# Two transformer blocks on one core: side work ordered by estimated readiness, and 64-row score products

## The chip, the cores and the metric

The kernel is one program on one NeuronCore of a Trainium2 chip. The metric is device time in microseconds (us) of one execution. The engines are called as in the profile: PE (TensorE, matrix products), PEld (its weight loads), DVE (VectorE), ACT (ScalarE), POOL (GpSimd), SP (SyncE, which only issues transfers here). A product has a stationary operand of up to 128 x 128 and a moving one of up to 512 columns; the result goes to a bank of PSUM.

## The reference, cut to what matters

Batch 1, 256 positions, width 2048, two different blocks, one after the other:

```
h = rms_norm(x)                       # block 1
aq, ak, av, hq, hf, hi, hg, gate_a, gate_b = split(h @ w_in)
y_attn = sliding_window_attention(rotary(aq), rotary(ak), av, sinks)  # 16 heads of 64, 4 kv heads, window 128
o = rms_norm(hgrn2_recurrence(silu(hq), hf, hi)) * silu(hg)           # 8 heads of 128
x = x + rms_norm((sigmoid(gate_a)*(y_attn@w_ab) + sigmoid(gate_b)*(o@w_hb)) @ w_out)
x = x + rms_norm((silu(gate) * up) @ w_down)                          # gate, up = rms_norm(x) @ w_gate_up
x = x + rms_norm((p @ w_ple_proj) * sigmoid(rms_norm(x) @ w_ple_gate))

proj = rms_norm(x) @ w_in_2           # block 2
score = sum over 16 index heads of w * relu(q_idx . k_idx / 8)        # heads of 64, top 64 keys of each row
a = softmax over the chosen keys, in a latent of 256                  # dsa, 8 heads of 128
b = causal softmax with a decay from cumulated log gates              # fox, 8 heads of 128
x = x + concat(a, b) @ w_o
x = rms_norm(x + conv_ffn(rms_norm(x)))
```

In the local attention a row of the first 128 positions sees 128 keys, a row of the second 128 sees 256, of which the window masks half. All inputs and results are fp32.

## The kernel before

**The main stream.** The large matrices are read in pieces of 512 KB (two times 128 rows by 512 columns) by transfers that SP issues. For each piece ACT rounds the numbers to the type fp32r (L283) and DVE forms what the rounding left off (L289); both go into a page called `ring`. A result tile (a bank named `mm`, 128 positions by 512 columns) is the sum of three products for each 128 rows of the matrix: rounded by rounded, rounded by rest, rest by rounded, all at L335 in `step`. `run` lays out in advance a list of steps of six such products each, gives each a planned time, and issues them one by one; the pieces of `ring` are made by a planned lead of about 12 us.

**The side work.** Everything between the large matrices (norms, rotary, local attention `swa`, the recurrence `hgrn`, gates, the indexer `head_iq`, `dsa`, `fox`) is written as Python generators. After each 1.4 us of planned time `run` calls `pump`, which advances every generator that is due by one piece. `yield 7` means "go on seven calls later". Nothing is reordered afterwards: the order in which the instructions are issued by this program is their order on each engine. So the yields decide where on PE a side product stands: an engine works its instructions in that order and waits where an operand is missing. Side products write to one of four banks named `sd`. They are plain fp32; transposes are done on PE too, against an identity matrix (`ident`).

**The waits.** All waits of the side work are fixed numbers of calls: `SWA_LEAD` 7, `Y_SOFT` 7 (between the softmax and the transposes of its result), `B_LEAD` 1, `FLIP_OUT` 5 and `FLIP_IN` 10 (around a turn of a tile through memory in the two feed-forward parts), and single numbers 2 to 7 elsewhere. Where the main stream itself needs a result of the side work that isn't yet written, `pump_until` calls `pump` until it is there.

**Local attention.** `swa` works one pair of heads after another, eight pairs. The keys are kept in `kz`, transposed, padded with zeros so that a product over all 128 rows gives one head of the pair in one half of its columns and the other in the other half: L626 gives the scores of the first 128 positions (256 columns for the pair), L627 of the second (512 columns). DVE scales and masks (L630, L632), takes maxima; ACT exponentiates; DVE divides by the sum (L653). After `Y_SOFT` calls six transposes (L660 to L662), two copies by ACT (L663, L664), and after three calls more the product with the values (L670 over 512 columns, L671 over 256), where each head uses one half of the result's rows.

**The indexer.** `head_iq` does the same for 16 index heads with one shared key: 16 blocks of one product each (256 or 512 columns), one bank and one ACT instruction for each, then DVE adds.

**Other lines.** L350 is a set of four transposes, L400 the evacuation that multiplies by a gain and rounds, L491 and L507 are small set-up products, L612 a copy of transposed queries. In `hgrn` L814 forms sums of logs on PE, L817 and L820 (POOL, 512 columns) and L821 (DVE) make its two operands, L827 uses them. L1349 gives the scores of `dsa` and `fox` in `softmax_pv`, L1352 their evacuation; L1244 is a set of transposes of block 2; L1428 cumulates the log gates from `nbf` (L1424). L963 and L997 lie at the end of the third large product of block 1, where the sum of squares of a whole row must be there before the next matrix can start.

## Time and profile before

| | us |
|---|---|
| median of 3 runs | 2660.38 |
| lowest and highest of them | 2657.01, 2662.94 |
| the profiled execution, its own time | 2657.43 |
| its span, first to last instruction | 2655.6 |
| PE busy in it | 2623.4 (99%) |
| DVE, ACT, POOL busy | 1613.8, 1339.5, 361.8 |

The granted clock of PE over the profiled execution was 0.998 of full speed. PE holds 11929 product records; one plain fp32 product is two records (it is done in two passes with two loads of weights), one fp32r product is one. A record's end is modelled and reaches past the start of the next; the time that a product takes is read from the start of one record to the start of a later one.

### The profile page before, as it was taken

The page shows a single profiled execution, that of the slowest core. Times are in us where ns is not written, and L with a number is a line of the kernel's source. Part 1 is how long each engine was busy: PE and PEld are TensorE (multiplying, and loading weights), DVE is VectorE, ACT ScalarE, POOL GpSimd, SP SyncE. Part 2 cuts the span into 40 slices and gives each one's busy share as a digit, 9 for nine tenths or more (in the row PEclk, how much of TensorE's full clock was granted, in tenths as well). Part 3 has the DMA queues.
Part 4 walks back from the last instruction along what each step waited for, and adds up shares of the span by engine and source line. Part 5 has one row for each costly group of instructions (what it writes and reads, how often), then busy time and mean ns, then how long its engine had stood idle before and what let it go on. Part 6 is the DMA issues. An engine that isn't in the chain of part 4 may idle for free.

```text
span 2655.6 us, 32471 instructions
## 1 busy us (share of the span) xinstructions
PE 2623.4 (99%) x11929; PEld 2168.9 (82%) x11929; DVE 1613.8 (61%) x2145; ACT 1339.5 (50%) x2004; POOL 361.8 (14%) x420
## 2 busy tenths in 40 slices
PE   8999999999999999999999999999999999999998
PEld 7887788888888888888887788788888888888887
DVE  6765676465555454545457564855557757575757
ACT  6545654454553443443435574554556636464644
POOL 1341031020100000000001110100013212121211
PEclk9999999999999999999999999999999999999999
DMA  7545445666676565656566666456556766575754
GB/s 256 165 129 171 161 147 185 221 230 243 219 243 219 212 210 206 217 201 223 209 209 220 235 213 184 137 175 214 191 198 235 250 221 237 209 242 207 246 202 146
DMA packets 154431, 547.02 MB, mean 206 GB/s; under 512 B 19512, under 2 KB 22096, under 8 KB 153248
## 3 DMA queue, kind: packets, MB, share of 16 engines
q1 hardware_dynamic: 133504, 476.83, 51.9%
q0 software_dynamic: 19472, 67.54, 7.8%
q8 instruction: 93, 1.52, 0.2%
q10 hardware_dynamic: 1296, 0.59, 0.1%
q14 instruction: 66, 0.54, 0.1%
HBM read 514.46 MB, written 30.43 MB: 205 GB/s over the span
## 4 chain that ended last, share of the span: by engine, by line
PE 95%; ACT 1%; DVE 1%; POOL 1%; issue 1%; DMA 0%; SPq 0%; ACTq 0%; POOLq 0%; DVEq 0%
PE mm L335 89%; PE sd L350 1%; PE sd L827 1%; DVE ring L289 1%; ACT ring L283 0%; PE sd L1272 0%; PE sd L1349 0%; POOL s L820 0%; ACT s L394 0%; PE sd L670 0%; PE sd L1381 0%; PE sd L627 0%; PE sd L1244 0%; DMA s<-in_x_dram 0%; PE sd L813 0%
## 5 line engine op out<-in xcount | busy, mean ns | idle before, releaser
L335 PE MATMUL mm<-ring,s 128*128 128x512 f32 (+1 forms) x10824 | 2508.7, 391 | 8.0 <-ACT ring L283 6.3
L335 PEld LDWEIGHTS mm<-ring,s 128*128 128x128 f32 x10824 | 2023.4, 188 | 430.8 <-ACT ring L283 7.6
L289 DVE TENSOR_TENSOR ring<-stg,ring 128x1024 fp32r<-128x1024 f32 (+1 forms) x904 | 1088.9, 1252 | 406.2 <-ACT ring L283 399.4
L283 ACT CAST ring<-stg 128x1024 fp32r<-128x1024 f32 (+1 forms) x904 | 904.5, 1049 | 159.3 <-PE mm L335 93.8
L370 POOL DMA_DIRECT2D flip<-s x66 | 37.0, 562 | 973.0 <-DVE s L366 967.4
L1231 ACT ACTIVATE s<-mm,ss 128x512 f32<-128x512 f32 x60 | 41.5, 691 | 237.6 <-PE mm L335 224.9
L1068 DVE TENSOR_TENSOR s<-mm,s 128x512 f32<-128x512 f32 x72 | 48.7, 687 | 86.5 <-PE mm L335 86.3
L1020 ACT ACTIVATE s<-mm,ss 128x512 f32<-128x512 f32 x22 | 15.2, 690 | 139.1 <-PE mm L335 139.1
L1033 DVE SCALAR_TENSOR_TENSOR s<-mm,ss,s 128x512 f32<-128x512 f32 x22 | 16.1, 730 | 108.3 <-PE mm L335 108.3
L345 POOL TENSOR_TENSOR small<-small,mhalf 128x1 f32<-128x1 f32 (+1 forms) x27 | 17.5, 649 | 361.3 <-DVE small L344 328.7
L820 POOL TENSOR_TENSOR s<-s,s 128x512 f32<-128x512 f32 x32 | 53.3, 1672 | 93.8 <-ACT s L817 89.1
L356 ACT CAST s<-sd 64x256 fp32r<-64x256 f32 (+2 forms) x34 | 16.0, 470 | 88.6 <-PE sd L350 49.7
L376 POOL DMA_DIRECT2D s<-flip x66 | 50.5, 767 | 67.8 <-DMA flip<-s 39.8
L394 ACT ACTIVATE s<-sd,cols 128x128 fp32r<-128x128 f32 x160 | 45.8, 388 | 22.0 <-PE sd L350 19.1
L357 DVE TENSOR_TENSOR s<-s,s 128x512 fp32r<-128x512 f32 x22 | 15.2, 690 | 65.3 <-ACT s L356 65.3
L1584 POOL TENSOR_TENSOR s<-s,s 128x512 f32<-128x512 f32 x22 | 41.2, 1874 | 82.9 <-DVE s L1567 82.8
L350 PE MATMUL sd<-ident,s 128*128 128x128 f32 x252 | 40.8, 285 | 9.9 <-DMA ident<-in_c_ident_dram 4.0
L350 PEld LDWEIGHTS sd<-ident,s 128*128 128x128 f32 x252 | 32.4, 147 | 20.7 <-DMA ident<-in_c_ident_dram 4.0
L1565 ACT ACTIVATE s<-s,cols 128x256 f32<-128x256 f32 x88 | 48.2, 594 | 1.5
L357 DVE TENSOR_TENSOR s<-sd,s 64x256 fp32r<-64x256 f32 (+2 forms) x34 | 18.7, 549 | 47.4 <-ACT s L356 47.3
L1587 ACT CAST s<-s 128x512 fp32r<-128x512 f32 x22 | 13.6, 620 | 66.7 <-POOL s L1584 66.7
L366 DVE STREAM_TRANSPOSE s<-s 128x512 f32<-128x512 f32 x66 | 46.2, 706 | 1.6
(293 smaller groups left out, 1247.4 us busy)
## 6 DMA issues: line engine op xcount, KB each, us to landing
stg<-in_w_in_dram SPq DMA_DIRECT2D x232, 512.0 KB, 4.4
stg<-in_w_gu_dram SPq DMA_DIRECT2D x176, 512.0 KB, 5.5
stg<-in_w_dn_dram SPq DMA_DIRECT2D x176, 512.0 KB, 5.4
stg<-in_w_up_dram SPq DMA_DIRECT2D x176, 512.0 KB, 5.3
flip<-s POOLq DMA_DIRECT2D x66, 256.0 KB, 2.6
s<-flip POOLq DMA_DIRECT2D x66, 256.0 KB, 5.7
stg<-in_w_out_dram SPq DMA_DIRECT2D x32, 512.0 KB, 5.7
stg<-in_w_pg_dram SPq DMA_DIRECT2D x32, 512.0 KB, 5.5
```

What stands on the lines that cost most here:

```text
L283: nc.scalar.copy(w[:, 0, :, 0 : cc.n], stg[n_hi][0][:, :, 0 : cc.n])
L289: nc.vector.tensor_tensor(wl[:, :, 0 : cc.n], unstage(n_lo)[:, :, 0 : cc.n], wh[:, :, 0 : cc.n].bitcast(F32), op=ALU.subtract)
L335: nc.tensor.matmul(c.ps[t][:, 0 : c.n], xl if p == "C" else xh, wl if p == "B" else wh, start=n == 0, stop=n == 6 * c.nhp - 1)
L350: self.nc.tensor.transpose(bank[:, a * P : (a + 1) * P], s, self.ident)
L366: nc.vector.transpose(ts, src)
L376: self.mq.dma_start(tr.rearrange("p (i x) -> p i x", i=4), d.rearrange("(i r) (j x) -> (r j) i x", i=4, j=4))
L394: nc.scalar.activation(hi[:, a], b3[:, a], AF.Copy, scale=g[a])
L820: nc.gpsimd.tensor_tensor(k3, d3, kt[:, None, :].to_broadcast([P, 4, P]), op=ALU.mult)
L1068: nc.vector.tensor_tensor(y, ps[t], y, op=ALU.add)
L1231: nc.scalar.activation(r, ps[t], AF.Copy, scale=self.rs[t])
L1565: nc.scalar.activation(v, u, AF.Identity, scale=w[2], bias=self.cols[:, C_CB + k : C_CB + k + 1])
L1584: nc.gpsimd.tensor_tensor(o, o, g, op=ALU.mult)
```

## The change

1. **Order by estimate.** Three new classes wrap the engines. While the program is issued they add up a cost for each instruction and keep, for each piece of a tile, an estimated time when it is written and read. A generator that used to yield a fixed number now yields 1 and then stays in `ripe(operands)` until the estimate for its operands is at most 0.3 us (`RIPE`) past the estimated time of PE (or of the engine named). `get("sd")` likewise waits until a bank is estimated free. Two ways around it: before the end of the set-up (`early`), and when the main stream has asked for a result for more than two calls (`rush`).
2. **Local attention in rounds of two pairs.** `kz` has no padding. A head's scores are a product over its own 64 rows; each pair has four products (128, 128, 256, 256 columns) into two banks. Two pairs follow each other, then all their 12 transposes into three banks, three ACT copies, and the product with the values as four products, each into 64 rows of the result, then one evacuation for both pairs.
3. **The indexer.** The same over 64 rows: one block of eight products of 128 columns and two of four products of 256 columns, for each half of the heads; six blocks instead of 16.
4. **Smaller.** No zeros are written and six transposes of padded keys are gone; two small transfers of `hgrn` are issued earlier; `softmax_pv` takes its two banks for transposes at once.

```
+RIPE = 0.3
+PATIENCE = 2
+class Watched:
...
+    def cost(self, op, out, ins, kw):
+        n = max(a.size() // max(1, a.shape[0]) for a in [out, *ins])
+        if op == "dma_start":
+            return (0.5, 1.9, out.size() * 4 / 340e3) if self.name == "SP" else (0.5, 4.3)
+        if self.name == "PE":
...
+                return n / 2400 + 0.0134 + back, 0.25
...
+            return (0.109 if op == "transpose" else 2 * max(0.109, r.size() // r.shape[0] / 1200)), 0.25
+        if self.name == "ACT":
+            return 0.15 + n / 1280 + (0.19 if "accum_out" in kw else 0.0), 0.15
+        if self.name == "DVE":
+            return 0.13 + n / 960, 0.15
+        return 0.3 + n / 450, 0.2
...
     def get(self, cls, n=1, dt=F32):
-        while not self.can(cls, n):
+        while not self.can(cls, n) or (cls == "sd" and not (self.rush or self.early) and not self.clk.free(cls, n)):
             yield 1
...
+    def ripe(self, *aps, eng="PE"):
+        while not (self.rush or self.early) and max(self.clk.there(a) for a in aps) > self.clk.now(eng) + RIPE:
+            yield 1
...
-            nc.tensor.matmul(p0, qt[:, 0:P], kz[:, q, :, 0:P], start=True, stop=True)
-            nc.tensor.matmul(p1, qt[:, P:256], kz[:, q, :, :], start=True, stop=True)
...
+                for t in range(2):
+                    for a, rows in enumerate(halves):
+                        nc.tensor.matmul(banks[a][:, P * t : P + 256 * t], qt[rows, P * t : P * t + P],
+                                         kz[rows, q, 0 : P + P * t], start=True, stop=True)
...
-            yield Y_SOFT
...
+            yield from self.ripe(l0, *l1)
...
-            nc.tensor.matmul(bo, v[:, 0], t0, start=True, stop=False)
...
+            for a, rows in enumerate(halves):
+                nc.tensor.matmul(bo[rows, :], v[:, 0, rows], ts[a], start=True, stop=False)
...
             bank = yield from self.get("sd")
             nc.vector.tensor_scalar(S["nbf"], lf, -1.0, None, op0=ALU.mult)
+            yield from self.ripe(S["nbf"])
...
-                    nc.tensor.matmul(b3, qts[p // 2][:, qs], kz[:, :, 0:n], start=True, stop=True)
...
+                        nc.tensor.matmul(bank[:, n * z : n * z + n], qts[p // 2][rows, qs], kz[rows, 0:n], start=True, stop=True)
```

**PE, second pair of the local attention, before.** `mm` is the main stream, `sd_1705` the product with the values of the pair ahead, `sd_1721` and `sd_1722` the scores of the next one.

```order
L335 MATMUL mm_1698<-ring_1609,s_4_99 128x512 x6
L670 MATMUL sd_1705<-s_174_1665,s_98_984 128x512
L671 MATMUL sd_1705<-s_174_1665,s_98_984 128x2x128
L335 MATMUL mm_1714<-ring_1609,s_4_99 128x512 x6
L626 MATMUL sd_1721<-s_98_984,s_79_816 128x256
L627 MATMUL sd_1722<-s_98_984,s_79_816 128x512
L335 MATMUL mm_1698<-ring_1625,s_4_99 128x512 x6
```

**PE, the first round of two pairs, after** (every instruction is recorded at line L116, that of the wrapper; `s_105_1031` are the queries, `s_162_1492` the keys, each product over 64 of their rows).

```order
L116 MATMUL mm_1513<-ring_1476,s_10_139 128x512 x6
L116 MATMUL sd_1583<-s_105_1031,s_162_1492 128x128
L116 MATMUL sd_1584<-s_105_1031,s_162_1492 128x128
L116 MATMUL sd_1583<-s_105_1031,s_162_1492 128x256
L116 MATMUL sd_1584<-s_105_1031,s_162_1492 128x256
L116 MATMUL mm_1522<-ring_1476,s_10_139 128x512 x6
L116 MATMUL sd_1616<-s_105_1031,s_162_1492 128x128
L116 MATMUL sd_1617<-s_105_1031,s_162_1492 128x128
L116 MATMUL sd_1616<-s_105_1031,s_162_1492 128x256
L116 MATMUL sd_1617<-s_105_1031,s_162_1492 128x256
L116 MATMUL mm_1513<-ring_1498,s_16_176 128x512 x6
```

Behind the last of these rows 42 more products of the main stream stand ahead of the round's 12 transposes; so 54 stand between the first scores and the transposes, where before 42 stood between a pair's scores and its transposes.

**DVE at the same place, after**, around the second pair's softmax: the first row here is the last of the first pair's ten, and no row of the main stream stands between the two pairs. `l03` is in the page `s_162_1492`, `l13` of this pair in `s_172_1574`.

```order
L116 TENSOR_SCALAR s_162_1492<-s_162_1492,small 128x256 x2
L116 SCALAR_TENSOR_TENSOR s_162_1492<-sd_1616,cm 128x128
L116 SCALAR_TENSOR_TENSOR s_172_1574<-sd_1616,cm 128x256
L116 SCALAR_TENSOR_TENSOR s_162_1492<-sd_1617,cm 128x128
L116 SCALAR_TENSOR_TENSOR s_172_1574<-sd_1617,cm 128x256
L116 TENSOR_REDUCE small<-s_162_1492 128x2
L116 TENSOR_REDUCE small<-s_172_1574 128x2
L116 TENSOR_TENSOR small<-small,rv 128x4 x2
L116 TENSOR_TENSOR small<-small 128x4
L116 RECIPROCAL small<-small 128x4
L116 TENSOR_SCALAR s_162_1492<-s_162_1492,small 128x128 x2
L116 TENSOR_SCALAR s_172_1574<-s_172_1574,small 128x256 x2
```

Before, a subtraction of the main stream (L289) stands behind each single pair's softmax.

**PE at the start of `dsa`, before** (`sd_12010` and `sd_12011` are the scores of the first pair of heads, `sd_12062` and `sd_12063` of the second; `ident` rows are transposes).

```order
L1349 MATMUL sd_12010<-s_1075_11361,s_1134_11872 128x128 x2
L1349 MATMUL sd_12011<-s_1075_11361,s_1134_11872 128x256 x2
L335 MATMUL mm_12031<-ring_11934,s_1015_10698 128x512 x6
L335 MATMUL mm_12040<-ring_11934,s_1015_10698 128x512 x6
L1244 MATMUL sd_12047<-ident,s_1143_11998 128x128 x4
L335 MATMUL mm_12031<-ring_11950,s_1015_10698 128x512 x6
L1349 MATMUL sd_12062<-s_1075_11361,s_1134_11872 128x128 x2
L1349 MATMUL sd_12063<-s_1075_11361,s_1134_11872 128x256 x2
```

**The same, after.**

```order
L116 MATMUL sd_11981<-s_1082_11359,s_1134_11864 128x128 x2
L116 MATMUL sd_11982<-s_1082_11359,s_1134_11864 128x256 x2
L116 MATMUL mm_11853<-ring_11902,s_1030_10775 128x512 x6
L116 MATMUL mm_11873<-ring_11902,s_1030_10775 128x512 x6
L116 MATMUL mm_11853<-ring_11923,s_1030_10775 128x512 x6
L116 MATMUL mm_11873<-ring_11923,s_1030_10775 128x512 x6
L116 MATMUL sd_12035<-ident,s_1145_11980 128x128 x2
L116 MATMUL sd_12036<-ident,s_1145_11980 128x128
L116 MATMUL sd_12035<-ident,s_1145_11980 128x128 x2
L116 MATMUL sd_12036<-ident,s_1145_11980 128x128
L116 MATMUL sd_12045<-s_1082_11359,s_1134_11864 128x128 x2
L116 MATMUL sd_12046<-s_1082_11359,s_1134_11864 128x256 x2
```

The second pair's scores stand behind 24 products of the main stream and the first pair's transposes, where before 18 products stood between the two.

## Rows read from the trace of the kernel before

**Rows 1.** The page's first part: busy us, share and instructions of each engine.

```profile
PE 2623.4 (99%) x11929; PEld 2168.9 (82%) x11929; DVE 1613.8 (61%) x2145; ACT 1339.5 (50%) x2004; POOL 361.8 (14%) x420
```

**Rows 2.** Groups of PE by form: busy us, mean ns, idle before.

```profile
L335 PE MATMUL mm<-ring,s 128*128 128x512 f32 x10728 | 2493.3, 392 | 8.0 <-ACT ring L283 6.3 <-DVE ring L289 1.5
```

**Rows 3.** The chain that ended last, its longest link: start, us, what.

```profile
1932.69 703.16 PE mm L335 x3102
```

**Rows 4.** Waits of PE from 30 to 2640 us: total us, times, longest.

```profile
PE mm L335 <- ACT ring L283: 6.3, 3, 3.7
PE sd L350 <- ACT ring L283: 2.1, 1, 2.1
PE sd L1349 <- DVE s L1352: 1.7, 1, 1.7
PE mm L335 <- DVE ring L289: 1.5, 2, 1.0
PE sd L827 <- POOL s L820: 1.1, 2, 0.6
PE sd L1428 <- DVE nbf L1424: 0.9, 1, 0.9
PE sd L670 <- ACT s L663: 0.9, 1, 0.9
PE sd L350 <- DVE s L997: 0.9, 1, 0.9
PE sd L626 <- ACT s L612: 0.5, 2, 0.3
```

**Rows 5.** Timeline of PE, 755 to 760 us: start, us, instructions.

```profile
754.62 2.88 PE L335 MATMUL mm<-ring,s 128*128 128x512 f32 x12
757.62 1.01 PE L507 MATMUL sd<-s 32*8 32x512 f32 x2
758.57 1.65 PE L335 MATMUL mm<-ring,s 128*128 128x512 f32 x6
```

**Rows 6.** Timeline of PE, 36 to 41 us.

```profile
35.69 2.89 PE L335 MATMUL mm<-ring,s 128*128 128x512 f32 x12
38.42 0.27 PE L491 MATMUL sd<-ident,s 128*16 128x128 f32 x1
38.45 1.63 PE L335 MATMUL mm<-ring,s 128*128 128x512 f32 x6
```

**Rows 7.** Timeline of PE in the local attention, 200 to 222 us.

```profile
203.37 1.02 PE L670 MATMUL sd<-s,s 128*128 128x512 f32 x2
204.23 0.59 PE L671 MATMUL sd<-s,s 128*128 128x256 f32 x2
...
206.05 0.59 PE L626 MATMUL sd<-s,s 128*128 128x256 f32 x2
206.48 1.02 PE L627 MATMUL sd<-s,s 128*128 128x512 f32 x2
...
216.91 0.27 PE L660 MATMUL sd<-ident,s 128*128 128x128 f32 x1
217.02 0.27 PE L661 MATMUL sd<-ident,s 128*128 128x128 f32 x1
```

**Rows 8.** Timeline of all engines, 204 to 222 us: the same pair on DVE.

```profile
206.68 0.42 DVE L630 SCALAR_TENSOR_TENSOR s<-sd,cm 128x256 f32<-128x256 f32 x1
...
211.79 1.01 DVE L653 TENSOR_SCALAR s<-s,small 128x128 f32<-128x128 f32 x4
```

**Rows 9.** Two stretches: us, busy by engine, clock, DMA share, GB/s.

```profile
1708.00:1712.00 4.00, 4.00 (x13) 3.13 (x12) 2.57 (x8) 3.24 (x10) 0.00 (x0) 0.57 0.60 205
1445.50:1448.50 3.00, 2.98 (x8) 2.32 (x9) 2.44 (x6) 1.21 (x4) 0.44 (x1) 0.50 0.40 87
```

**Rows 10.** Timeline of all engines, 1436 to 1447 us.

```profile
1441.56 0.68 DVE L963 TENSOR_TENSOR s<-mm,s 128x512 f32<-128x512 f32 x1
...
1445.52 2.08 PE L335 MATMUL mm<-ring,s 128*128 128x512 f32 x4 [3.72 <-ACT ring L283]
```

**Rows 11.** Timeline of all engines in the recurrence, 90 to 98 us.

```profile
92.36 1.81 POOL L820 TENSOR_TENSOR s<-s,s 128x512 f32<-128x512 f32 x1 [4.92 <-ACT s L817]
...
95.28 2.27 POOL L820 TENSOR_TENSOR s<-s,s 128x512 f32<-128x512 f32 x1
```

More of the change, by code (lines that the diff above doesn't have):

```diff
@@ L48, with __init__, blocks, there @@
 N_COLS = 171 + 3 * 88
+class Clock:
+    def __init__(self):
+        self.t = {"PE": 0.0, "ACT": 0.0, "DVE": 0.0, "POOL": 0.0, "SP": 0.0, "DMA": 0.0}
+        self.wrote, self.read = {}, {}
+        self.banks = {"sd": [0.0] * 4, "mm": [0.0] * 4}
+        self.side = False
+    @staticmethod
+    def blocks(ap):
+        name, dims = ap.tensor.name, list(ap.ap)
+        if ap.space == DRAM:
+            lo, step = ap.offset, 8192
+        else:
+            lo, step, dims = ap.offset % max(1, dims[0][0]), 64, dims[1:]
+        hi = lo + sum((n - 1) * abs(d) for d, n in dims)
+        return [(name, b) for b in range(lo // step, hi // step + 1)]
+    def there(self, ap, eng=None):
+        return max(t + (0.0 if e == eng else late) for t, late, e in (self.wrote.get(k, (0.0, 0.0, eng)) for k in self.blocks(ap)))
+    def now(self, eng):
+        return max(self.t[eng], self.t["PE"])
+    def note(self, eng, outs, ins, cost, late, dma=0.0):
+        begin = self.t[eng]
+        for ap in (*ins, *outs):
+            begin = max(begin, self.there(ap, eng))
+        keys = [k for ap in outs for k in self.blocks(ap)]
+        for k in keys:
+            begin = max(begin, self.read.get(k, 0.0))
+        end = self.t[eng] = begin + cost
+        if dma:
+            end = self.t["DMA"] = max(self.t["DMA"], end) + dma
+        for ap in ins:
+            for k in self.blocks(ap):
+                self.read[k] = max(self.read.get(k, 0.0), end)
+        for k in keys:
+            self.wrote[k] = (end, late, "DMA" if late > 1.0 else eng)
+    def give(self, cls, n):
+        self.banks[cls] += [max(self.t["ACT"], self.t["DVE"])] * n
+        self.banks[cls].sort()
+    def free(self, cls, n):
+        return self.banks[cls][n - 1] <= self.t["PE"] + RIPE
+    def take(self, cls, ap):
+        t = self.banks[cls].pop(0)
+        for k in self.blocks(ap):
+            self.wrote[k] = (t, 0.0, None)
@@ new lines, with __init__, __getattr__, call @@
+class Watched:
+    def __init__(self, clock, name, eng):
+        self.clock, self.name, self.eng = clock, name, eng
+    def __getattr__(self, op):
+        f = getattr(self.eng, op)
+        def call(out, *args, **kw):
+            aps = [a for a in (*args, *kw.values()) if isinstance(a, bass.AP)]
+            outs = [out] + [kw[k] for k in ("accum_out",) if k in kw]
+            ins = [a for a in aps if a is not kw.get("accum_out")]
+            self.clock.note(self.name, outs, ins, *self.cost(op, out, ins, kw))
+            return f(out, *args, **kw)
+        return call
+    def cost(self, op, out, ins, kw):
[3 more added lines that the diff above has]
+        if self.name == "PE":
+            r = ins[-1]
+            back = 0.0
+            if r.dtype == F32R:
+                back, self.clock.side = (0.09 if self.clock.side else 0.0), False
+                return n / 2400 + 0.0134 + back, 0.25
+            self.clock.side = True
+            return (0.109 if op == "transpose" else 2 * max(0.109, r.size() // r.shape[0] / 1200)), 0.25
[4 more added lines that the diff above has]
+        return 0.3 + n / 450, 0.2
@@ L51, with __init__ @@
+class Chip:
+    def __init__(self, nc, clock):
+        self.tensor = Watched(clock, "PE", nc.tensor)
+        self.scalar = Watched(clock, "ACT", nc.scalar)
+        self.vector = Watched(clock, "DVE", nc.vector)
+        self.gpsimd = Watched(clock, "POOL", nc.gpsimd)
+        self.sync = Watched(clock, "SP", nc.sync)
 class XT:
@@ new lines, in swa @@
+            for a, rows in enumerate(halves):
+                nc.tensor.matmul(bo[rows, :].rearrange("p (u t n) -> p u t n", u=2, t=2)[:, :, 1, :], v[:, 1, rows],
+                                 ts[2][:, 256 * a : 256 * a + 256].rearrange("p (u n) -> p u n", u=2), start=False, stop=True)
+            self.drop(*ts)
+            self.evac_split(bo.rearrange("p (u n) -> p u n", u=2), self.ya.hi(q)[:, 2 * p2 : 2 * p2 + 2, :],
+                            self.ya.lo(q)[:, 2 * p2 : 2 * p2 + 2, :])
@@ L821, in hgrn @@
                     nc.vector.tensor_tensor(q3, d3, qt[:, None, :].to_broadcast([P, 4, P]), op=ALU.mult)
-                    yield 3
+                    yield 1
+                    yield from self.ripe(dk, dq, *(() if half else (qk,)))
                     s = yield from self.get("sd")
@@ L994, in boundary @@
         r = self.rstd(tot, 1, D)
-        yield B_LEAD
+        yield 1
+        yield from self.ripe(r, *xs, eng="DVE")
         for j in range(4):
@@ L1036, in done @@
             ts, d = yield from self.flip_out(g)
[L1037 removed]
+            yield 2
+            yield from self.ripe(d, eng="POOL")
             tr = yield from self.flip_in(d)
@@ L1044, in done @@
                 yield 1
-            yield FLIP_IN
+            yield 2
+            yield from self.ripe(tr, eng="ACT")
             s = slice(t * P, (t + 1) * P)
@@ L1375, in softmax_pv @@
         self.drop(l0, l1)
-        yield 3
+        yield 1
         if need is not None:
             yield from need()
+        yield from self.ripe(t0, t1[:, 0:256], *(v(z, a) for z in range(2) for a in range(2)))
         bo = yield from self.get("sd")
@@ L1493, in pair @@
                                   bass.AP(tensor=self.d_cum.tensor, offset=self.d_cum.offset + 256 * (h + a), ap=[[0, P], [1, 256]]))
-            yield 3
+            yield 1
+            yield from self.ripe(row, eng="DVE")
             cur = self.cm[:, P:256]
```

242 lines of the change are left out of this document (129 added, 113 removed).

## The prediction, made before the result was known

> **What bounds the kernel now.** I read the page's first part first: PE is busy for 99% of the span, the next engine for 61% [rows 1]. The chain of work that ended last says the same in time: its longest link is 3102 products of the main stream in 703.16 us, one after the other [rows 3], 0.2267 us each. There are 10728 of them [rows 2], so 10728 x 0.2267 = 2432 us of the 2655.6; the other 224 us hold the shorter products of the main stream, the side products, the start and the end, and the waits below. So PE bounds nearly everywhere; the time changes only by what PE's own row of instructions costs and by its waits. What ACT, DVE and POOL save (fewer copies, no zeros) counts only where PE waits for them.
>
> The waits are then read one by one [rows 4]. Those for the pieces of the matrices (6.3 and 1.5) and the one behind L997 (0.9) lie at the three or so boundaries between large matrices; the other six lines are side products whose operand is late, 2.1 + 1.7 + 1.1 + 0.9 + 0.9 + 0.5 = 7.2 us. At the beginning of `dsa` and at the end of the third large product the clock is low as well, 0.57 over 4 us and 0.50 over 3 us [rows 9]: 0.43 x 4 = 1.7 us and 0.50 x 3 = 1.5 us are lost beside the waits. That is the lower of the two levels mixed with the full one, directly behind a wait of PE (3.72 us before 1445.52 [rows 10]).
>
> The sum is made against the profiled execution, 2657.4 us. The median of the runs is 3.0 above it, so 3.0 is added at the end. A measurement of this kernel can tell about 0.2%, 5.3 us, from no change.
>
> **(a) Products over 64 rows or into 64 rows.** A plain fp32 product takes two records: 0.86 us for 512 columns (203.37 to 204.23), 0.43 for 256 (206.05 to 206.48) [rows 7]. A record of 128 columns or fewer takes 0.11, as the transposes show (216.91 to 217.02 [rows 7]). Before, 24 products of 512 and 24 of 256 columns do the scores of `swa`, its products with the values and the indexer: 24 x (0.86 + 0.43) = 30.9 us. After, the same columns are spread over twice as many products of half the rows: 32 of 128 columns (0.22 each), 32 of 256, and eight each of 512 and 256 in the products with the values, 7.0 + 13.8 + 6.9 + 3.4 = 31.1. One after the other they gain nothing (0); if two that use different halves of the array always run beside each other, half of it is gone (-15.4). No row of before shows two such products. I take the middle, from the order: each product has two records that use the same half, so I let them follow each other, and only the second record of one can lie beside the first of the next. For the 256-column scores of `swa` that is 0.21 in each of 8 pairs (1.7); for the indexer's four products of 256 three such overlaps in each of 4 blocks, 0.64 x 4 = 2.6; for the products with the values 0.43 + 0.43 in each of 4 rounds, 3.4; nothing for 128 columns, which stay at the floor. **-7.7**, bounds -15.4 and 0.
>
> **(b) Changes of shape.** The new products work on another tile of the array than the full products on both sides. The nearest rows: two records over a tile of 32 x 8 between full products [rows 5]. From 754.62 to 758.57 are 3.95 us; 12 products and one of 512 columns make 12 x 0.2267 + 0.86 = 3.58. So 0.37 us is lost there. A small tile of 128 x 16 loses nothing: 35.69 to 38.45 is 2.76, and 12 x 0.2267 = 2.72 [rows 6]; it keeps all 128 rows. There are 18 blocks of the new shape (8 of scores, 6 of the indexer, 4 products with the values): 0 to 18 x 0.37 = 6.7. Scores cut rows like the first row, so 14 x 0.37 = 5.2; the products with the values keep 128 rows and cut columns, between the two rows, so 4 x 0.18 = 0.7. **+5.9**, and it can't be below zero, since nothing is gained by a switch. [...]
>
> **(c) Six transposes fewer:** 6 x 0.11 = **-0.7**. The rest of the main stream on PE is the same number of products with the same shapes. The copies, zeros and small transfers that go or move lie on ACT, DVE and POOL, with 50%, 61% and 14% [rows 1]: nothing, as long as no wait for them is on PE's row; (d) prices that. In the two feed-forward parts the turned tiles are now waited for by estimate: no wait for them in [rows 4] and pieces made 12 us ahead, so nothing; if an estimate there is early, ACT stands at its queue and the pieces behind it come later, for which the 12 us are the cover.
>
> **(d) Side waits.** The 7.2 us and the 1.7 of clock at `dsa` = 8.9 go if the estimates hold: the order after has the second pair's scores of `dsa` 24 products later instead of 18, and the scores wait for their operands rather than for a count of calls. New waits come instead. The estimate lets an instruction go up to 0.3 us early, and calls are 1.4 us apart: a gate that opens at a random place in that interval waits 0.3 x 0.3 / (2 x 1.4) = 0.03 us on average, some 70 gates, 2.3 us. POOL is under-estimated: 0.3 + 512/450 = 1.44 us and 0.2 more for the hand-over, where the rows show 1.81 and 2.27 [rows 11], mean 2.04: 0.4 short, with the 0.3 together 0.7, so 0.7 x 0.7 / 2.8 = 0.18 us at each of 32 places in `hgrn`, 5.6. Between 0 and 7.9 I take 3.0: the 2.3, and an eighth of POOL's, because even the fixed waits of before, which are no longer than needed at two of these places, cost 1.1 in all [rows 4]. 3.0 - 8.9 = **-5.9**, bounds -8.9 and -1.0.
>
> Behind a side product that waits, PE's whole queue stands, the main stream first; so each microsecond of such a wait is one of the total.
>
> **(e) Boundaries.** 6.3 + 1.5 + 0.9 of waits and 1.5 of clock lie there. At 1441.56 DVE takes in the last tile of the row and everything behind it is a chain through the norm, until PE starts at 1445.52 [rows 10]. In the new order one group of L400 instead of two stands ahead of L963 and the main stream still starts the same products behind it; the chain itself is not shorter. I take **-2.0**, bounds 0 and -5.0 (the 8.7 of waits without the 3.72).
>
> **The sum:** -7.7 + 5.9 - 0.7 - 5.9 - 2.0 = -10.4, 2647.0 on the profiled execution, **2650** on the median. Its own range, with one term at an end: 2643 to 2657.
>
> **The rivals.**
>
> *A: the halves run fully side by side and a switch costs nothing.* For it: within a block nothing else stands between them, and they go to two banks. Against it: [rows 5]. -15.4 - 0.7 - 5.9 - 2.0 = -24.0: 2633.4 + 3.0, **2636**. [...]
>
> *B: they run one after the other, and the switch costs.* For it: the rows of before show every product starting after the one ahead, 0.86 and 0.43 apart. 0 + 5.9 - 0.7 - 5.9 - 2.0 = -2.7: 2654.7 + 3.0, **2658**. That the change does not do what its products say is this case.
>
> *C: the estimates are early as often as the fixed waits were,* POOL's above all: (d) at -1.0 and (e) at 0, the rest as forecast. -10.4 + 4.9 + 2.0 = -3.5: **2657**.
>
> *D, slower: the rounds of `swa` come too late.* One softmax takes DVE 206.68 to 212.80, 6.1 us [rows 8], and has 4.1 us to spare before its transposes at 216.91. In a round two of them follow each other on DVE with two more evacuations each, about 6.4 us each. From the first scores' start to the transposes lie two blocks of scores and 54 main products, 1.3 + 54 x 0.2267 + 1.3 = 14.8 us; DVE begins 1.3 after that start and needs 12.8, so 0.7 is left. The exponentials of ACT lie inside these times, and a rounding of a piece stands on ACT for about 1 us (the same engine, between them). If two or three of those stand ahead, the transposes wait, some 2.8 us, and the clock falls behind the wait as in [rows 9], 1.7: 4.5 x 4 rounds = 18. 2657.4 - 10.4 + 18 + 3.0 = **2668**. It decides from 0.7 us of delay on; to bring the time over that of before by more than 0.2% it takes 15.7 us over the forecast, 3.9 in each round: 2.2 of wait and the 1.7 of clock. The estimate counts ACT and DVE too, and so should open the gate later; that speaks against it.
>
> **How the numbers follow.** Forecast 0.42, A 0.25, B 0.17, C 0.08, D 0.08. The likeliest gives 2650. The range reaches from below A to above B, 2632 to 2663, and leaves out D and the outer parts of A. Faster by over 0.2% means below 2655.1: forecast and A (0.67) and the faster fifth of B and C, 0.72. Slower means above 2665.7: D and a little of B, 0.09. Within 0.2%: 0.19.
>
> **What would show it.** In the trace of after: (a) the start of the second product of a pair's scores lies less than 0.43 us behind the first one's (if at once, A; if 0.43, B). (b) From the last main product ahead of a block of scores to the first one behind it, 0.37 more than the records make. (d) The waits of PE list holds about 3 us of side waits, no line of `dsa`'s scores among them and POOL's as the largest; the stretch at the start of `dsa` is at full clock. (e) The wait at the end of the third product of block 1 is still some 3 us. D would show as a wait for DVE ahead of the first transposes of each round. The prediction is wrong if the products of 64 rows take more than their columns say, or if main products beside them slow down, which no row of before can exclude.

## The result and the profile after

The changed kernel takes 2731.34 us (median; 2729.13 to 2732.19), the kernel before on the same chip 2661.66: a ratio of 1.0264 with a 95% interval of 1.0251 to 1.0277. The forecast was 2650, the range 2632 to 2663. It is slower by 70 us, on the other side of before.

The page's first part after, beside [rows 1]: PE is still busy for 97%, but of a span of 2729.8 us.

```profile
PE 2646.0 (97%) x11987; PEld 2169.2 (79%) x11987; DVE 1599.3 (59%) x2149; ACT 1339.5 (49%) x1986; POOL 359.5 (13%) x413
```

PE's waits from 30 to 1930 us (total us, times, longest; the first five of nine lines), the answer to [rows 4]:

```profile
PE sd L116 <- DVE s L116: 11.3, 11, 4.6
PE sd L116 <- POOL s L116: 2.9, 6, 1.0
PE mm L116 <- ACT ring L116: 2.8, 3, 1.0
PE mm L116 <- DVE ring L116: 2.6, 3, 1.1
PE sd L116 <- DMA s<-in_p_dram: 1.1, 1, 1.1
```

And from 1930 us to the end, the second block's feed-forward part, where the kernel before has no wait of PE at all:

```profile
PE mm L116 <- DVE ring L116: 36.3, 23, 3.9
PE mm L116 <- ACT ring L116: 8.4, 5, 2.5
```

The two windows of 2000 to 2100 us, first before, then after (columns as in [rows 9]):

```profile
2000.00:2100.00 100.00, 100.00 (x443) 82.84 (x442) 75.04 (x84) 62.96 (x92) 32.07 (x32) 1.00 0.68 241
```

```profile
2000.00:2100.00 100.00, 85.89 (x343) 67.85 (x342) 61.07 (x71) 52.78 (x77) 23.36 (x24) 0.93 0.56 192
```

In the same 100 us PE does 343 products instead of 443, and its clock is 0.93: it stands at 0.50 for 3.4 us from 2035.9, for 3.4 from 2059.8 and for 6.8 from 2087.1, each time within 2.5 us of the end of one of the three longest waits of the window (1.65, 3.67 and 3.83 us). Laid side by side by the number of main products done, after is 6.4 us late at the 7800th of 10872 (1950 us before) and 74.2 us late at the end. So **67.8 us of the loss arise in the convolution's feed-forward part (`conv`)**, 44.7 of them as listed waits and the rest mostly as lower clock (0.98 over the 800 us from 1930 on, 1.00 before), and 6.4 ahead of it.

### The profile page after: what moved, and what is told of

Same layout as the page of the kernel before. It is cut to its first block, busy times and chain, and to the rows that moved or that the text cites. A ratio compares the mean times of both kernels' runs of the same rounds, so it can differ in the third digit from the quotient of the medians.

```text
span 2729.8 us, 32554 instructions
## 1 busy us (share of the span) xinstructions
PE 2646.0 (97%) x11987; PEld 2169.2 (79%) x11987; DVE 1599.3 (59%) x2149; ACT 1339.5 (49%) x1986; POOL 359.5 (13%) x413
## 3 DMA queue, kind: packets, MB, share of 16 engines
q8 instruction: 94, 1.54, 0.2%
## 4 chain that ended last, share of the span: by engine, by line
PE 70%; DMA 9%; DVE 7%; issue 6%; ACT 5%; POOL 3%; ACTq 0%; SPq 0%; POOLq 0%; DVEq 0%
PE mm L116 66%; DMA s<-flip 5%; DVE s L116 5%; PE sd L116 4%; ACT s L116 3%; DMA flip<-s 3%; POOL s L116 2%; DVE ring L116 2%; ACT ring L116 2%; DMA stg<-in_w_in_dram 1%; ACT L116 0%; DMA s<-in_x_dram 0%; POOL flip L116 0%; DMA s<-in_p_dram 0%; POOL small L116 0%
## 5 line engine op out<-in xcount | busy, mean ns | idle before, releaser
L116 PE MATMUL mm<-ring,s 128*128 128x512 f32 (+1 forms) x10824 | 2522.9, 393 | 51.2 <-DVE ring L116 38.8
L116 PEld LDWEIGHTS mm<-ring,s 128*128 128x128 f32 x10824 | 2030.9, 189 | 489.1 <-DVE ring L116 49.1
L116 DVE TENSOR_TENSOR ring<-stg,ring 128x1024 fp32r<-128x1024 f32 (+1 forms) x904 | 1083.5, 1247 | 333.6 <-ACT ring L116 332.8
L116 ACT CAST ring<-stg 128x1024 fp32r<-128x1024 f32 (+1 forms) x904 | 904.0, 1048 | 164.1 <-PE mm L116 44.6
L116 ACT ACTIVATE s<-mm,ss 128x512 f32<-128x512 f32 x134 | 92.0, 686 | 321.9 <-PE mm L116 299.6
L116 DVE TENSOR_TENSOR s<-mm,s 128x512 f32<-128x512 f32 x104 | 70.5, 688 | 161.0 <-PE mm L116 124.8
L116 POOL DMA_DIRECT2D flip<-s x66 | 37.2, 564 | 965.1 <-DVE s L116 960.7
L116 POOL TENSOR_TENSOR s<-s,s 128x512 f32<-128x512 f32 (+2 forms) x76 | 128.5, 1695 | 220.5 <-ACT s L116 181.6
L116 DVE SCALAR_TENSOR_TENSOR s<-s,cols,s 128x255 f32<-128x255 f32 (+1 forms) x132 | 72.8, 572 | 116.5 <-ACT s L116 114.1
L116 ACT COPY s<-s 128x256 f32<-128x256 f32 x88 | 33.5, 404 | 204.1 <-DMA s<-flip 194.7
L116 DVE TENSOR_TENSOR s<-s,s 128x512 f32<-128x512 f32 (+1 forms) x88 | 74.6, 853 | 98.2 <-ACT s L116 98.1
L116 ACT CAST s<-s 128x512 fp32r<-128x512 f32 (+1 forms) x49 | 30.9, 630 | 206.3 <-DMA s<-flip 161.9
L116 ACT ACTIVATE s<-s 128x512 f32<-128x512 f32 x107 | 67.0, 633 | 126.1 <-DVE s L116 124.3
L116 PE MATMUL sd<-ident,s 128*128 128x128 f32 x431 | 67.4, 284 | 18.1 <-DVE s L116 9.3
L116 DVE SCALAR_TENSOR_TENSOR s<-mm,ss,s 128x512 f32<-128x512 f32 x22 | 16.1, 730 | 113.2 <-PE mm L116 113.2
L116 PEld LDWEIGHTS sd<-ident,s 128*128 128x128 f32 x431 | 53.8, 145 | 34.8 <-issue 10.7
L116 PE MATMUL sd<-s,s 128*128 128x128 f32 (+7 forms) x432 | 76.4, 345 | 1.3 <-DVE s L116 0.9
L116 DVE STREAM_TRANSPOSE s<-s 128x512 f32<-128x512 f32 x66 | 46.5, 707 | 50.6 <-ACT s L116 46.0
L116 DVE SCALAR_TENSOR_TENSOR s<-s,cols 128x255 f32<-128x255 f32 (+1 forms) x44 | 20.3, 482 | 84.6 <-ACT s L116 83.8
L116 POOL TENSOR_TENSOR s<-s 128x512 f32<-128x512 f32 (+1 forms) x28 | 42.6, 1520 | 192.4 <-DVE s L116 171.6
L116 PEld LDWEIGHTS sd<-s,s 128*128 128x128 f32 (+2 forms) x432 | 54.7, 189 | 16.4 <-issue 7.2
L116 ACT ACTIVATE s<-sd,cols 128x128 fp32r<-128x128 f32 (+1 forms) x170 | 50.0, 390 | 30.1 <-PE sd L116 25.6
```

The source lines that it names most:

```text
L116: return f(out, *args, **kw)
```

## Where the loss in conv comes from

ACT's waits from 1930 us on, the longest line, and the transfers that POOL issues (KB each, median us from issue to landing), both of after:

```profile
ACT s L116 <- DMA s<-flip: 194.7, 44, 9.7
```

```profile
flip<-s POOLq DMA_DIRECT2D x66, 256.0 KB, 3.5
s<-flip POOLq DMA_DIRECT2D x66, 256.0 KB, 6.9
```

and the transfers of before:

```profile
flip<-s POOLq DMA_DIRECT2D x66, 256.0 KB, 2.6
s<-flip POOLq DMA_DIRECT2D x66, 256.0 KB, 5.7
```

In `conv` before, ACT waits for no turned tile; after, it stands 195 us at its queue, once for each of 44 turned tiles, which come in 22 pairs. The timeline of one pair, rows of all engines that bear on it:

```profile
2034.85 20.98 PE L116 MATMUL mm<-ring,s 128*128 128x512 f32 x84 [0.76 <-DVE ring L116]
2036.49 3.88 ACT L116 CAST ring<-stg 128x1024 fp32r<-128x1024 f32 x4
2036.85 0.56 POOL L116 DMA_DIRECT2D flip<-s  x1 [18.03 <-DVE s L116]
2037.66 0.56 POOL L116 DMA_DIRECT2D flip<-s  x1 [0.26 <-DVE s L116]
2041.81 0.76 POOL L116 DMA_DIRECT2D s<-flip  x1 [3.59 <-issue]
2044.38 0.76 POOL L116 DMA_DIRECT2D s<-flip  x1 [1.81 <-DMA flip<-s]
2049.09 0.41 ACT L116 COPY s<-s 128x256 f32<-128x256 f32 x1 [8.72 <-DMA s<-flip]
2051.04 0.41 ACT L116 COPY s<-s 128x256 f32<-128x256 f32 x1 [1.54 <-DMA s<-flip]
2052.48 1.04 ACT L116 CAST ring<-stg 128x1024 fp32r<-128x1024 f32 x1
2055.50 2.80 DVE L116 SCALAR_TENSOR_TENSOR s<-s,cols,s 128x255 f32<-128x255 f32 x4 [1.47 <-ACT s L116]
2056.38 1.04 ACT L116 CAST ring<-stg 128x1024 fp32r<-128x1024 f32 x1
2058.23 3.43 DVE L116 TENSOR_TENSOR ring<-stg,ring 128x1024 fp32r<-128x1024 f32 x2
2059.49 5.75 PE L116 MATMUL mm<-ring,s 128*128 128x512 f32 x17 [3.67 <-DVE ring L116]
```

ACT rounds four pieces (2036.49 to 2040.37) and stands at the copy of the first turned tile for 8.72 us, at the second for 1.54. The next piece is rounded at 2052.48: 12 us without one. Those 12 are about the whole lead of the pieces here. DVE loses time too: four operations of `conv` that ACT's late copies feed (2055.50) stand on it ahead of the subtraction of that piece, which starts only at 2058.23. So PE runs dry at 2055.8, for 3.67 us; its next 17 products take 5.75 where 17 x 0.2267 = 3.9. From the first turn's issue (2036.85) to the last landing (2051.04) are 14.2 us. The estimate gives four legs of 0.5 for the issue and 4.3, two after two: some 10.

The feed-forward part of block 1 has such a gate too, and there the same wait costs nothing. ACT's waits for turned tiles from 30 to 1930 us, first before, then after:

```profile
ACT s L356 <- DMA s<-flip: 56.3, 9, 13.9
```

```profile
ACT s L116 <- DMA s<-flip: 161.9, 20, 17.6
```

Yet from the 3000th to the 5000th main product, all in that part, after stays 6.6 us late throughout. What differs is the lead: for instance no piece is rounded from 902.5 to 922.6 us while PE goes on without a wait, because, counting 12 products to a piece, the last piece ahead of that gap is first used some 29 us after it was rounded.

## The experiments

Times are medians; the ratio with its interval is against the kernel before on the same chip, whose median was 2661.0 to 2662.7 in all of them.

| run | us | ratio | 95% |
|---|---|---|---|
| flip_fixed | 2661.98 | 1.0005 | 0.9996 to 1.0015 |
| flip_cost | 2674.98 | 1.0048 | 1.0033 to 1.0063 |
| act_time | 2668.20 | 1.0025 | 1.0016 to 1.0034 |
| before_early | 2750.65 | 1.0336 | 1.0315 to 1.0356 |
| products | 2665.14 | 1.0015 | 1.0006 to 1.0024 |
| products7 | 2650.73 | 0.9963 | 0.9948 to 0.9978 |
| order_only | 2664.99 | 1.0015 | 1.0006 to 1.0024 |
| hgrn_fixed | 2662.03 | 1.0003 | 0.9993 to 1.0012 |
| est | 2640.90 | 0.9926 | 0.9909 to 0.9942 |
| est_table | 2643.14 | 0.9934 | 0.9920 to 0.9949 |
| est_pool | 2643.11 | 0.9933 | 0.9918 to 0.9948 |
| ripe_late | 2647.70 | 0.9942 | 0.9927 to 0.9957 |
| est_flip | 2644.60 | 0.9939 | 0.9924 to 0.9953 |
| est_old | 2643.68 | 0.9928 | 0.9912 to 0.9945 |

**conv: the wait undone, its price, its clock.**

```
flip_fixed, in conv:
-            yield 2
+            yield 5
             for ts, d in ds:
-                yield from self.ripe(d, eng="POOL")
...
-            yield 2
-            yield from self.ripe(*trs, eng="ACT")
+            yield 10
flip_cost: a transfer of POOL
-            ... else (0.5, 4.3)
+            ... else (0.5, 7.0)
act_time: the gate of ACT's copies
-            yield from self.ripe(*trs, eng="ACT")
+            while not (self.rush or self.early) and max(self.clk.there(a) for a in trs) > self.clk.t["ACT"] + RIPE:
+                yield 1
```

> The changed kernel with one thing undone: in the convolution's feed-forward part (conv) the turned tiles are waited for by the fixed 5 and 10 calls of before, not by the estimate. Theory 1 (the copies by ACT are issued too early, ACT stands 195 us at its queue for the turned tiles, the pieces of the matrices behind them come late): ACT waits for the turned tiles fall from 195 us to under 10, PE's waits for pieces behind 1930 us from 45 us to under 3, the time by 66: about 2665. Rival (the loss there comes from the other gates, such as the one on the banks, or from memory traffic): less than 20 us come back, over 2710.

> The changed kernel with one number changed: a transfer that POOL issues is estimated at 7.0 us instead of 4.3 (the trace of after has 6.6 to 6.9 to landing). Theory 1a (only this price is wrong): all of the loss in conv returns, about 2665 as with the fixed waits. Theory 1b (the gate compares the estimate with PE's time, but ACT works some 7 us ahead of PE there, since it makes pieces 12 us ahead; so ACT still reaches the copy early by that lead): ACT still waits 3 to 5 us at each of the 22 pairs of tiles, 70 to 110 us in all instead of 195, and PE gets back about half: 2685 to 2705.

> The changed kernel with the gate ahead of ACT's copies in conv measured against the estimated time of ACT alone, not against the later of ACT and PE; the price of the transfer stays 4.3. Theory 1b: the lead is taken out, what is left is the price, about 2 to 3 us for each of 22 pairs of tiles, 50 to 70 us of ACT waits in place of 195, nearly all within the lead of the pieces: 2665 to 2680. Theory 1a (only the price is wrong): little changes, over 2710.

With the fixed waits back the whole loss in conv is gone: PE has no wait behind 1930 us, ACT has this one left, and the run is as fast as before.

```profile
ACT s L116 <- DMA s<-flip: 0.6, 1, 0.6
```

With the right price alone (flip_cost), ACT and PE have these left from 1930 us on:

```profile
ACT s L116 <- DMA s<-flip: 28.4, 11, 3.8
```

```profile
PE mm L116 <- DVE ring L116: 2.9, 5, 0.6
```

By main products, flip_cost loses 4.5 us in conv instead of 67.8. So theory 1a, the price, holds, and 1b as I stated it (70 to 110 us of ACT waits left, half the loss) does not. The price counts twice, since the read-back stands behind a gate of its own and is issued late: 2 x 2.7 us. act_time keeps the price and moves the gate by ACT's lead; it loses 7.2 there, so either margin takes most of the loss away, and the lead of the pieces swallows small waits. flip_cost is still 13 us slower than flip_fixed, most likely because the same price also moves two transfers of `hgrn`: it is 16.3 late at the end of the recurrence already, flip_fixed 6.1, and the difference of 10 arises between 85 and 125 us, where `hgrn` starts. No run has that price for these two alone.

```
before_early, the kernel before, in conv:
-            yield FLIP_OUT
+            yield 2
-            yield FLIP_IN
+            yield 4
```

> The kernel before with two numbers changed, in conv alone: 2 calls in place of 5 ahead of reading a turned tile back, 4 in place of 10 ahead of ACT's copies, which is about what the estimate left (5.4 us behind the read). No estimate, no new products. Theory (copies issued ahead of the landing hold ACT's queue, the pieces behind them come late, PE waits): ACT waits for turned tiles 150 to 220 us in all, PE for pieces 30 to 50, the time 2710 to 2735. Rival (that loss needs the gates of the change): under 2675.

The mechanism alone, put into the kernel before, does more than the whole change did (+89 us). ACT's and PE's waits from 1930 us on:

```profile
ACT s L1560 <- DMA s<-flip: 214.7, 42, 10.7
```

```profile
PE mm L335 <- DVE ring L289: 49.1, 22, 3.9
PE mm L335 <- ACT ring L283: 5.5, 5, 2.6
```

**The products.** `products` is the kernel before with `swa`, `head_iq` and the key parts of after, every `ripe` left out, a fixed number of calls in its place:

```
products                                   products7
 yield Y_SOFT    # ahead of the transposes  the same
 yield 4         # ahead of the values      yield 7
                                            yield 2 more ahead of head_iq's transposes
```

> The kernel before with the new products alone: rounds of two pairs of heads, products over 64 rows in the local attention and the indexer, no padded keys; all waits stay fixed numbers of calls (7 behind the second pair's softmax, 4 ahead of the products with the values), no estimate anywhere. The trace of after has a pair's scores at 1.06 us in place of 1.29 (8 times), a round's products with the values at 1.7 in place of two times 1.29 (4 times), the indexer's blocks at 7.6 in place of 10.6 in all, and six transposes less: -1.9 - 3.5 - 3.0 - 0.7 = -9. Theory: 2653, faster by 0.3%. Rival (rounds of two pairs are too long for DVE and PE waits for the second softmax): within 0.1% of before.

> As the run `products` (the kernel before with the new products alone, waits fixed), with 7 calls in place of 4 between a round's transposes and its products with the values, and two calls more ahead of the indexer's transposes: in `products` PE waited 6.3 us there for ACT's copies and 3.0 us for a copy ahead of the indexer's transposes, and the clock fell behind the longest wait. Theory (the products are worth 9 us, those waits hid it): both waits gone, about 2652, 0.3% faster than before. Rival (rounds cost as much as the products save, in a way the list of waits does not show): 2658 or more.

`products` came out slower than before, against the theory, and its list of waits (30 to 2640 us) says why; they are waits that my own numbers of calls put in, ahead of the products with the values (L668) and the indexer's transposes (L1239):

```profile
PE sd L668 <- ACT s L661: 6.3, 2, 5.6
PE sd L1239 <- ACT s L1226: 3.0, 2, 1.8
```

Later by a few calls (products7), both lines are gone and the products show their worth: 10.6 us, against 9 expected. The rounds of two pairs are not too long for DVE.

How the new products run, on PE's timeline of after (the changed kernel), against [rows 7]:

```profile
216.30 0.93 PE L116 MATMUL sd<-s,s 64*128 64x128 f32 x8
217.16 1.66 PE L116 MATMUL mm<-ring,s 128*128 128x512 f32 x6
...
240.23 1.51 PE L116 MATMUL sd<-s,s 128*64 128x512 f32 x8
241.67 23.46 PE L116 MATMUL mm<-ring,s 128*128 128x512 f32 x102
```

A pair's eight records take 0.86 from their start to that of the next main product, part of the change of shape included; one after another they would take 4 x 0.11 + 4 x 0.215 = 1.30. In the trace the records of the two halves start in pairs, 7 ns apart: they run fully side by side. Around them, from the last main product ahead to the third behind, 0.41 us are lost more than the records make, for each block of scores, 0.36 for the products with the values. That is about the 0.37 of [rows 5]. In sum: 18 blocks cost 22.9 us where 32 cost 31.2 before, 8.3 less.

**The other gates.** What is left in flip_fixed: products worth 9 us, and yet no gain. order_only puts the products of before back into flip_fixed (its lines are shown against the kernel before), hgrn_fixed puts hgrn's fixed waits back:

```
order_only, in swa (and the same in head_iq, head_kv, head_small)
-            yield Y_SOFT
+            yield 1
+            yield from self.ripe(l0[:, 0:256], l1)
hgrn_fixed, in hgrn
-                    yield 1
-                    yield from self.ripe(dk, dq, *(() if half else (qk,)))
+                    yield 3
...
```

> flip_fixed with the products of before: one pair of heads after another over all 128 rows, padded keys, 16 blocks of the indexer, each with a gate by estimate in place of the fixed calls. So it is the order by estimate alone, without the loss in conv. Theory (products -9, gates ahead of the side products +12, boundaries -4): 9 us over flip_fixed less what single pairs wait less, 2667 to 2672. Rival (new products cost as much as they save): 2659 to 2664, as flip_fixed.

> flip_fixed with the fixed waits of before inside hgrn (3 calls ahead of its score products, 2 ahead of the two last steps); all else by estimate. Theory (most of the 6.1 us that flip_fixed is behind at the end of the recurrence comes from gates in hgrn): PE's waits for DVE and POOL before 460 us fall from 9.5 us to about 2, the low clock at 390 us goes, 2653 to 2656. Rival (they come from the local attention's rounds): under 2 us change.

order_only: 2664.99, between theory and rival; 5.9 us late against flip_fixed at the end of the recurrence, 5.2 at the end. hgrn_fixed changes nothing in the time, as the rival said, but not for the rival's reason: waits move within the stretch (PE's waits for DVE 10.5 instead of 11.2, with a new one of 3.98 at 184.05), so no single place holds the loss.

One place in full, the start of `dsa` in after; before, the transposes wait for nothing there:

```profile
1690.37 9.01 DVE L116 TENSOR_TENSOR ring<-stg,ring 128x1024 fp32r<-128x1024 f32 x4
1690.53 6.63 POOL L116 TENSOR_TENSOR s<-s,s 128x1024 f32<-128x1024 f32 x2 [9.80 <-DVE s L116]
1693.69 5.84 PE L116 MATMUL mm<-ring,s 128*128 128x512 f32 x24
1699.30 0.41 DVE L116 SCALAR_TENSOR_TENSOR s<-sd,s 128x256 f32<-128x256 f32 x1
1700.27 1.28 ACT L116 ACT_TABLE_LOAD   x1 [15.80 <-DVE small L116]
1704.10 1.41 PE L116 MATMUL sd<-ident,s 128*128 128x128 f32 x6 [4.57 <-DVE s L116]
```

Four subtractions take 9.01 us on DVE while POOL works on two large operations. Their mean, 2.25, which the expectations below use, hides two kinds: their single records last 1.22, 3.40, 3.42 and 1.21 us, and the two long ones each started while an operation of POOL was under way. Alone one takes 1.22 (at 215.07 in the same trace). Behind them the softmax starts at 1699.30, ACT first loads a table for 1.28, and PE stands for 4.57 at the transposes. The estimate has 0.13 + 1024/960 = 1.20 for the subtraction and nothing for the load. `est` corrects this; est_table and est_pool each have a part:

```
est, in note and cost (with conv's fixed waits as in flip_fixed)
+        if eng == "DVE" and self.t["POOL"] > begin:
+            cost *= 1.6
...
+            late = 1.28 if new != self.table else 0.0
...
-        return 0.3 + n / 450, 0.2
+        return 0.35 + n / 300, 0.2
est_table: the second alone; est_pool: the first and third alone
ripe_late (with the old prices, flip_fixed)
-RIPE = 0.3
+RIPE = -1.0
```

> The run flip_fixed with three corrections of the estimate: POOL at 0.35 + n/300 us in place of 0.3 + n/450, DVE 1.6 times as long while POOL is estimated busy (the trace of after has four subtractions at 2.25 us each beside POOL where one alone takes 1.22), and 1.28 us where ACT changes its table of functions (22 such loads in the trace, none in the estimate). Theory (the gates ahead of the side products open early because of these three): PE's waits for DVE and POOL at side products fall from 14.1 us in flip_fixed to under 5, the 4.6 at the start of dsa among them, and the time to about 2652. Rival (they open early for another reason, such as the time at which the program was laid out against the real one): within 3 us of flip_fixed, 2659 to 2665.

> Of the three corrections in `est` only ACT's table loads (1.28 us); POOL at its old price and DVE without the slow-down beside POOL; conv's waits fixed. If the loads were the main error: 2641 to 2648. If DVE beside POOL and POOL's price were: 2655 to 2662, with the 4.6 us wait at the start of `dsa` still there in part.

> Of the three corrections in `est` only POOL's price and DVE's slow-down beside POOL, no table loads; conv's waits fixed. If these were the main error: 2641 to 2648, the wait at the start of `dsa` down from 4.6 us to under 1.5. If the table loads were: 2655 to 2662.

> flip_fixed with one number changed: a gate opens when the estimate is at least 1.0 us in the past (RIPE -1.0), not up to 0.3 us ahead; all prices as in the change. Theory A (what the corrections did is to make the gates later; any correction of about a microsecond does it): 2640 to 2648. Theory B (the gates must be later at the right places, those with a table load or with POOL beside DVE): 2652 to 2662.

est is the fastest of all, 2640.90, 0.74% under before and 21 us under flip_fixed. PE's waits at side products in est, est_table and est_pool, in this order:

```profile
PE sd L120 <- POOL s L120: 2.1, 1, 2.1
PE sd L120 <- DVE s L120: 0.7, 2, 0.5
```

```profile
PE sd L118 <- DVE s L118: 4.4, 6, 1.9
PE sd L118 <- POOL s L118: 0.6, 2, 0.3
```

```profile
PE sd L120 <- DVE s L120: 2.5, 4, 1.8
PE sd L120 <- POOL s L120: 2.3, 4, 0.7
```

All three are at 3 to 5 us, from 14.1 in flip_fixed; either half of the correction does nearly all of it, so neither error can be called the cause, and both of my expectations that one of the two would be without effect failed. ripe_late settles why: with the wrong prices, but all gates 1.3 us later, 14 of the 21 us come back (16 if each run is put against the kernel before on its own chip). What the gates lacked was a margin. The right prices are worth another 5 to 7 us over a blind one by the medians; the two intervals in the table overlap.

**The whole change with right prices, and the order without the products.** est_flip is est with conv's gates too, and 7.0 us for a turned tile's transfers; est_old is est with the products of before.

> The whole change with all its gates, conv's too, and only the estimate corrected: the three corrections of `est`, and 7.0 us in place of 4.3 for a transfer that turns a tile through memory. Theory (order by estimate is sound, its prices were wrong): within 5 us of `est`, 2640 to 2646, faster than before by 0.6 to 0.8%. Rival (fixed waits are needed in conv): ACT waits at its queue for turned tiles by over 50 us and over 10 us are lost behind 1930 us, 2651 or more.

> `est` with the products of before (one pair after another over 128 rows, 16 blocks of the indexer): order by a corrected estimate alone. Theory (the new products are worth 9 to 10 us on PE whatever the order): 2649 to 2652, so about 10 of the 20 us come from the products and 10 from the order. Rival (the products are worth less, as the 3 us between order_only and flip_fixed say): 2643 to 2646.

est_flip: 2644.60, so the change as such, every gate by estimate, is 0.6% faster than before once its prices fit. est_old: 2643.68; the rival's figure. On PE's row the products save 9 us, yet beside a good order they bring 2.8 in the medians (1.4 with each put against before on its own chip; the intervals overlap nearly whole) and 1.5 in the profiled spans. Part of the rest is two waits of est that est_old does not have: PE waits 1.41 us for a piece at 319.14, and 2.15 for POOL at 403.42, with the clock low behind the second,

```profile
403.00:409.00 6.00, 5.58 (x22) 4.60 (x23) 3.51 (x5) 2.65 (x4) 2.16 (x2) 0.72 0.27 87
```

0.28 x 6 = 1.7 more, 5.3 in all. One to two us of it I can't place. Each change of the order deals out such waits anew: that is what the runs show, and no run holds the order fixed while the products change. So the products' own share in the 20 us of est stays open.

## Why the prediction was wrong, point by point

**The step that failed** stands under (c): "no wait for them in [rows 4] and pieces made 12 us ahead, so nothing". I named the danger in the same sentence (ACT stands at its queue, the pieces behind it come late) and took the 12 us as the cover without a sum. The sum was to be had: the diff states 4.3 us for a transfer of POOL, the transfers of before show 5.7 for the read-back, and the fixed waits there were 5 and 10 calls of 1.4 us, 21 us, in place of an estimate of some 10. A stall of up to 10 us on the engine that makes the pieces, 22 times in 700 us, uses up a lead of 12. No rival had this; flip_fixed, flip_cost and before_early show it: 67.8 us in `conv`, none with the fixed waits. For the other feed-forward part, in block 1, the step held: ACT waits there 161.9 us for turned tiles, and PE pays nothing. And [rows 4], which the step rests on, lists PE's waits alone; whether ACT stands, and how long, is in ACT's own waits: before, 56.3 us at turned tiles in block 1 and none in `conv`.

**(a)** was mis-sized: -15.4, not the -7.7 taken. The halves run side by side in full (rival A's half of it). My reading that the two records of a product follow each other before the next may start is refuted by the starts 7 ns apart.

**(b)** held: +5.9 forecast, about 18 x 0.4 = 7.2 measured. So (a) and (b) together, block by block, are -8.3 in place of -1.8.

**(d)** had the wrong sign. I let the waits of before go and took 3.0 for new ones; flip_fixed has 14.1 at DVE and POOL in place of the 7.2, and each costs about 0.16 more than the list says (at 112.49 in after 0.55 is listed, where 0.82 lie between the starts of two records and 0.11 is what the first one takes: 0.71 lost; the same 0.16 at 88.12 and 97.31), and the low clock behind the longer ones (0.84 from 1690 to 1712 us in flip_fixed, with the wait of 4.6). The missed terms were a margin in the gates, the table loads and DVE beside POOL. The table loads had no term in the diff's cost; DVE beside POOL was in the trace of before ("94.64 3.99 DVE L289", two subtractions, in the window of [rows 11]). Only POOL's own price was seen.

**(e)** held in size: the boundaries gain 3.4 us (order_only between the 5700th and the 6600th main product), -2.0 was taken. What was to show it did not: the wait was to be "still some 3 us", and in place of the 3.72 of [rows 10] stand two, of 0.7 and 1.0. The 3.4 is no firm number either. before_early issues the same instructions as before up to `conv` and has the same waits here, yet is 2.9 us later over this boundary, by the clock; before, then before_early:

```profile
1450.00:1460.00 10.00, 10.00 (x52) 8.25 (x51) 8.98 (x22) 6.22 (x22) 0.52 (x1) 1.00 0.82 288
```

```profile
1450.00:1460.00 10.00, 10.00 (x47) 8.18 (x46) 8.13 (x18) 5.66 (x20) 0.77 (x2) 0.85 0.69 233
```

**Rival D** did not come: in the round at 216 us the second softmax ends on DVE at 229.7 and the transposes start at 232.0 without a wait. **C** was the right direction for (d) but priced at 7.9 of waits, without conv.

With the measured sizes of (a), (b), (c) and (e), and (d) as est leaves it (2.8 of side waits in place of 7.2), the sum is -8.3 - 0.7 - 3.4 - 4.4 = -16.8; the profiled span of est is 16.0 shorter than that of before, 2639.6 against 2655.6, its median 20.5. That the sum comes so close is in part luck: it takes the products at their full 9 us, of which est against est_old shows at most 2.8, and it leaves out the clock behind the waits. Of the 4.5 between the two measured figures 3.9 lie in before, whose profiled execution was that much under its median.

## What to carry to other kernels

Where a cost model sets the order of in-order queues, put the price of each step beside a row of the trace before believing it, transfers first, and give every gate a margin: in these runs an instruction that came a microsecond late cost little while other work stood ahead (ripe_late: gates 1.3 us later, 14 us under flip_fixed), one that came early held up everything behind it (before_early: 89 us over before). An edit may be taken at nothing only after the cover is put against the largest stall and its number of repeats. Measure the lead where the stall will be: in `conv`, with about 12 us, it hid nearly all of ACT waits of up to 3.8 us (flip_cost), not ones of 10 us every 30; in block 1, where the pieces lay some 29 us ahead at the place shown, it hid waits of 17.6.

## What the runs showed of the hardware

In after, two plain fp32 products on different halves of PE's rows, or into different halves of its columns, start 7 ns apart and run together (216.30, 240.23); entering and leaving that shape costs 0.41 us for a block of scores and 0.36 for one of products with the values. DVE's subtraction of 128 x 1024 takes 1.22 us alone and 3.40 to 3.42 when it starts behind one of POOL's 128 x 1024 operations, which themselves take 3.3 to 3.4 there; the one that started ahead of POOL's operation (1690.37) took its 1.22. POOL's of 128 x 512 take 1.29 alone and up to 2.3 beside DVE. So both engines lose in these places; why, no run shows. ACT's 23 table loads in after took 1.283 us each. And the clock behind a wait differed where the instructions were the same: behind the wait at the end of the third large product (3.72 us in before) the stretch from 1450 to 1460 us had 1.00 in before and 0.85 in before_early.
